# Per-token sums of squares: blocks of 32 ones stand still, the squares move through four column strips, the sums pass through memory as rows

## Chip, cores and metric

One core of one Trainium2 chip. The metric is the device time of one execution in microseconds (us), the median of the runs shown; fewer is better.

## The reference

One layer of a decoder trunk on 1024 tokens of width 1024: a gated mixer branch, a Mamba-2 (SSD) branch, and a merge of both. What matters here is the end of the SSD branch. Its output `y_b`, 2048 values per token, is multiplied with a gate and then normalised in 8 groups of 256 values, each by the root of its own mean square:

```python
y_b = ssd_scan(xh, dt, a, bm, cm) + xh * d_skip[:, None]
yz = (y_b.reshape(b, s, SSM_D_INNER) * silu(ssm_z)).reshape(b, s, SSM_GROUPS, 256)
y_b = rms_norm(yz, ssm_norm_w.reshape(SSM_GROUPS, -1))    # yz * rsqrt(mean(yz*yz) + EPS) * w
merged = sigmoid(g_a) * (y_a @ w_proj_a) + sigmoid(g_b) * (y_b @ w_proj_b)
return x + gate * (merged @ w_out)
```

So for each of the 8 groups and each of the 1024 tokens one number is wanted: the inverse root of a mean of 256 squares.

## The kernel before

Activations lie transposed: 128 channels on the partitions, tokens along a row. A group of 256 channels is a tile `yz` of two halves j, each 128 channels by 512 tokens, and there are two such tiles per group, q = 0 and 1 (first and second 512 tokens).

The SSD stage runs 32 steps. `order` lists them as pairs of groups that take turns: (0,0), (1,0), (0,1), (1,1) and so on, four steps s of 256 tokens per group, then the next pair of groups. A step has three items, `front`, `back` and `prep`, and after each item `run_tasks` starts whatever was put off with `later(delay, ...)` for that many items. Between the items, matrix products of another branch (`proj_a`, tiles `pma`) are drawn in to fill TensorE. `fetch` loads the next step's `sl` and `dcy`; there are 5 sets of these buffers. Matmuls (`mm`, L81), transposes (`tp`, L84) and the loads on the SP queue (`load`, L90) keep the order in which they are written; stores go out on ScalarE's queue (`store`, L93) and these, with the instructions of VectorE (V), ScalarE (A) and GpSimd (G), are placed by a scheduler that works by its own estimate of times.

After every second step of a group, `post` (L1078) stores `yz` to `yb_d`, puts off `squares` by 5 items (in place: ScalarE squares both halves, GpSimd adds them) and `post2` by 17. `post2` (L1098) sums over the 128 channels on TensorE: each 128x128 block of squares is loaded as weights and one column of ones moves through it, so that the tokens come out on the partitions, one column per block, and L1104 makes the mean and adds EPS for 128x4 values into `ssq`. After the second half L1108 takes the power -0.5 of the group's 8 columns on GpSimd. Eight items later `post3` (L1112) transposes these 8 columns on TensorE into 8 rows, VectorE copies them out, and a store writes them to `rs_d`.

Groups 6 and 7 end last. Their second halves are done beside the first product `p1` of the next stage: `late.post2` follows unit 1 and unit 4 of `p1` with both halves of the squares unadded (tiles `sq`, so 16 instead of 8 matmul instructions), and `post3` follows units 4 and 6. There, `rows_bank` hands out the accumulators `yp` that the product `p5` takes over afterwards.

The next stage multiplies the normalised `y_b` with `w_proj_b` in units of 12 matmuls, order p1, p5, p2, p3, p6, p7, p4. `y_load` broadcasts `rs_d` to `rb` and loads `yb_d` to `yn`, 6 units ahead; `y_norm` (L1403) and the splits (L1442 to L1448) follow 4 units ahead.

One more place uses narrow weights already, at the start of the kernel, in `matvec` (tile `pm`): 32-wide weights, written to four strips of 32 partitions:

```python
mm(pm[32 * q : 32 * q + 32, 0:256], scz[:, i, :], aw[n][:, i].rearrange("p j c -> p (j c)"), i < 4, i >= 4)
```

In the trace a float32 matmul shows as two instructions (two passes).

Of the kernel before, what the change touches and what calls it, by code (L numbers as in the profile page):

```python
# [12 lines left out]
ALU = mybir.AluOpType  # L13
# [3 lines left out]
P = 128  # L17
D = 1024
S = 1024
KT = D // P  # L20
NCH = S // P
NG = 8
# [3 lines left out]
EPS = 1e-6  # L26
# [9 lines left out]
def hybrid_kernel(  # L36
# [7 lines left out]
    V, A, G, PE = nc.vector, nc.scalar, nc.gpsimd, nc.tensor  # L44
# [8 lines left out]
    def dt_(shape, name):  # L53
        return dram.tile(shape, F32, name=name, tag=name)

    acs_d = dt_([NG, 4, HPG, 256], "acs_d")
    rs_d = [dt_([1, S], f"rs_d{g}") for g in range(NG)]
    v_d = dt_([NG, P, NCH * P], "v_d")
    ya_d = [dt_([P, S], f"ya_d{g}") for g in range(NG)]
    mt_d = [dt_([P, S], f"mt_d{g}") for g in range(NG)]  # L60
# [9 lines left out]
    def cst(shape, name, dt=F32):  # L70
        return const.tile(shape, dt, name=name, tag=name)
# [8 lines left out]
    def mm(acc, l, r, first=True, last=True):  # L80
        pin(PE.matmul(acc, l, r, start=first, stop=last))  # L81

    def tp(dst, src, idn):
        pin(PE.transpose(dst, src, idn))  # L84
# [4 lines left out]
    def load(dst, src):  # L89
        pin(nc.sync.dma_start(dst, src))  # L90

    def store(dst, src):
        nc.scalar.dma_start(dst, src)  # L93

    ident = cst([P, P], "ident")
    make_identity(nc, ident)
    ones = cst([P, P], "ones")
    G.memset(ones, 1.0)
    tri = cst([P, P], "tri")
    G.affine_select(out=tri, in_=ones, compare_op=ALU.is_ge, fill=0.0, base=0,  # L100
                    pattern=[[1, P]], channel_multiplier=-1)
    nhalf = cst([P, NCH], "nhalf")
# [13 lines left out]
    cwt = cst([P, P], "cwt")  # L116
# [9 lines left out]
    ssq = cst([P, NG * NCH + 24], "ssq")  # L126
# [356 lines left out]
    def later(delay, f, *a):  # L483
        tasks.append((slot[0] + delay, f, a))
# [474 lines left out]
    class Group:  # L959
# [136 lines left out]
            G.tensor_add(sq[0], sq[0], sq[1])  # L1096

        def post2(self, q, sq):  # L1098
            g = self.g
            pq = rows_bank[0](f"pq{g}_{q}")  # L1100
            for i in range(4):
                for j, t in enumerate(sq):
                    mm(pq[:, i : i + 1], t[:, i * P : (i + 1) * P], ones[:, 0:1], j == 0, j == len(sq) - 1)
            V.tensor_scalar(ssq[:, g * NCH + q * 4 : g * NCH + q * 4 + 4], pq[:, 0:4], 1.0 / 256, EPS,  # L1104
                            op0=ALU.mult, op1=ALU.add)
            if q == 1:
                c8 = slice(g * NCH, (g + 1) * NCH)
                G.tensor_tensor(ssq[:, c8], ssq[:, c8], nhalf, op=ALU.pow)  # L1108
                if g < NG - 2:
                    later(8, self.post3)  # L1110

        def post3(self):  # L1112

            g = self.g
            pr = rows_bank[0](f"pr{g}")
            tp(pr[0:NCH, 0:P], ssq[:, g * NCH : (g + 1) * NCH], ident)
            row = (cwt, tri)[g % 2][0:NCH, :]
            V.tensor_copy(row, pr[0:NCH, 0:P])
            store(rs_d[g].rearrange("o (c p) -> (o c) p", p=P), row)

    groups = [Group(g) for g in range(NG)]
    rows_bank = [bank]
# [233 lines left out]
    def banks(name, c):  # L1356
        return [psb.tile([P, 512], F32, name=f"{name}{j}", tag=f"b{c}{j}") for j in range(4)]
# [99 lines left out]
    def multiply(u, ps):  # L1457
        nm, k = units[u]
        first = nm in ("p1", "p5", "p2", "p3")
        a, (bh, bl) = aops.pop(u), bops.pop(u)  # L1460
        for j in range(4):
            js = slice(j * P, (j + 1) * P)
            for n, (v, r) in enumerate(((0, bh), (0, bl), (1, bh))):
                pin(PE.matmul(ps[j], a[:, v, js], r, start=first and n + k == 0, stop=n == 2 and k == KT - 1,  # L1464
                              skip_group_check=not first))
# [3 lines left out]
    def gate_load(b, h):  # L1469
        hs = slice(h * 512, (h + 1) * 512)  # L1470
        th, ma = gate_slot(f"tg{b}_{h}"), gate_slot(f"ma{b}_{h}")
        load(th, th_d[(KT + b) * P : (KT + b + 1) * P, hs])
        load(ma, mt_d[b][:, hs])
        gates[b, h] = th, ma
# [105 lines left out]
    for u, (nm, k) in enumerate(units):  # L1580
        if k == 0:
            if nm == "p1":
                psy = banks("yp5", "y")
                psx = banks("x", "x")
                rows_bank[0] = lambda name: psy[("pr6", "pr7", "pq6_1", "pq7_1").index(name)]
            elif nm in ("p2", "p3"):
                psy = banks(f"y{nm}", "y")
            elif nm == "p6":
                room.extend(rb_r[0])
            ps = psy if nm in ("p2", "p5", "p3") else psx  # L1590
        multiply(u, ps)
        ahead(u)
        if nm == "p1" and k in (1, 4):
            late = groups[NG - 2 + k // 4]
            late.post2(1, late.late)
        if nm == "p1" and k == 4:
            for tags, _ in (y1_r, ym_r):
                room.extend(tags)
        if nm == "p1" and k in (4, 6):
            groups[NG - 4 + k // 2].post3()  # L1600
        if k % 2 and nm in GATES:
            gate_load(GATES[nm][0] + k // 2, GATES[nm][1])
        if nm == "p4":
            for at, f, a in BESIDE:
                if at == k:
                    f(*a)
        if k % 2 and more and nm not in ("p2", "p5"):
            merged(*more.pop(0))
        if k == KT - 1:
            for j in range(4):  # L1610
                with tc.high_priority():
                    if nm == "p1":
                        t = slot_tile(f"c11_{j}")
                        A.copy(t, psx[j])
                        more.append((j, 0, t, f"c11_{j}"))
# [184 lines left out]
```

## Time and profile before

| | |
|---|---|
| time, median of 3 runs | 1409.17 us (1408.26 to 1411.2) |
| profiled execution, its own time | 1411.01 us |
| its span | 1409.2 us |
| TensorE busy / VectorE / ScalarE / GpSimd | 98% / 75% / 57% / 15% of the span |
| granted TensorE clock, mean | 0.998 |
| SSD stage in the trace | about 950 to 1162 us |
| product p1 | 1162 to 1189 us |

Busy time of TensorE counts overlapping matmuls once, and the ends of matmuls are modelled; the distance from one start to the next says more. PE is TensorE's matmuls, PEld its weight loads, DVE is VectorE, ACT ScalarE, POOL GpSimd, and SPq and ACTq are the queues on which SyncE and ScalarE issue transfers.

### The profile page before, as it was taken

To read this page: it belongs to the slowest core of one execution; us is meant where nothing else is said; L and a number is where in the kernel's file an instruction comes from. 1 tells how busy PE (TensorE), PEld (TensorE's weight loads), DVE (VectorE), ACT (ScalarE), POOL (GpSimd) and SP (SyncE) were. 2 spreads that over 40 slices of the span, in tenths; PEclk is the share of its full clock that TensorE was granted. 3 is DMA by queue.
4 is the path that set the end of the run, shared out by engine and by line. 5 is a ranking of instruction groups with operands and counts; after the bars stand their busy time and mean duration, and the time that the engine had idled before them with its cause. 6 is when DMAs were issued, how large, how long until landed. Compare 5 with 4: busy or idle time off the path is not lost. (4 is left out here: it accounts for less than half of the span.)

```text
span 1409.2 us, 20659 instructions
## 1 busy us (share of the span) xinstructions
PE 1380.6 (98%) x7051; PEld 1146.3 (81%) x7051; DVE 1061.2 (75%) x1863; ACT 796.5 (57%) x1471; POOL 213.7 (15%) x208
## 2 busy tenths in 40 slices
PE   8999999999999999999999999999999999999997
PEld 6788888888888888888888888888887887878886
DVE  4686677767868899788898786378677757875976
ACT  5664576656566655555566555586776723322443
POOL 0000000000000011000100010037778850000001
PEclk9999999999999999999999999999999999999999
DMA  8552433333444667877766874498788759878903
GB/s 265 150 162 82 148 98 107 110 109 105 131 136 141 179 198 238 256 232 229 219 196 175 250 221 120 165 337 310 260 283 278 268 193 333 322 232 296 359 26 120
DMA packets 271918, 283.13 MB, mean 201 GB/s; under 512 B 14300, under 2 KB 222596, under 8 KB 271812
## 3 DMA queue, kind: packets, MB, share of 16 engines
q1 hardware_dynamic: 184548, 198.39, 44.1%
q10 hardware_dynamic: 87264, 83.41, 17.6%
q8 instruction: 56, 0.92, 0.3%
q14 instruction: 50, 0.41, 0.1%
HBM read 194.42 MB, written 87.33 MB: 200 GB/s over the span
## 5 line engine op out<-in xcount | busy, mean ns | idle before, releaser
L780 POOL TENSOR_TENSOR wog<-wog,gb 128x256 f32<-128x256 f32 x16 | 18.0, 1140 | 672.4 <-DMA wog<-in_w_out_dram 672.4
L994 ACT ACTIVATE dcy<-dcy,nacs 128x128 f32<-128x128 f32 x256 | 78.6, 388 | 15.5 <-POOL dcy L989 14.5
L989 POOL TENSOR_SCALAR_AFFINE_SELECT dcy<-dcy 128x1024 f32<-128x1024 f32 x32 | 35.4, 1105 | 139.6 <-ACT ea L986 135.8
L907 ACT ACTIVATE ac<-ac 128x1024 f32<-128x1024 f32 x32 | 33.9, 1060 | 25.0 <-DVE ac L905 24.8
L986 ACT ACTIVATE ea<-dcy 64x512 f32<-64x512 f32 x64 | 40.1, 626 | 13.7 <-DMA dcy<-acs_d 13.3
L81 PE MATMUL pma<-yh,wah 128*128 128x512 f32 x128 | 43.3, 419 | 0.0
L81 PE MATMUL pma<-yh,wal 128*128 128x512 f32 x128 | 42.6, 413 | 0.0
L1076 POOL TENSOR_TENSOR yz<-y,sl 128x512 f32<-128x512 f32 x32 | 41.4, 1293 | 1.1
L1014 DVE TENSOR_TENSOR dcy<-dcy,pc 128x1024 f32<-128x1024 f32 x32 | 38.9, 1216 | 3.3 <-PE pc L84 1.9
L81 PE MATMUL pma<-yl,wah 128*128 128x512 f32 x128 | 40.1, 394 | 0.0
L1074 DVE TENSOR_TENSOR ym<-yn,ea 128x512 f32<-128x512 f32 (+1 forms) x32 | 19.9, 621 | 26.6 <-PE yn L81 26.5
L1075 POOL TENSOR_TENSOR y<-y,ym 128x512 f32<-128x512 f32 (+1 forms) x32 | 36.6, 1142 | 13.6 <-DVE ym L1074 13.5
L81 PEld LDWEIGHTS yn<-sl,st 128*128 128x128 f32 x224 | 30.4, 190 | 9.0 <-POOL yz L1076 3.6
L81 PE MATMUL yn<-sl,st 128*128 128x128 f32 x224 | 31.7, 277 | 5.5 <-DVE st L1044 5.5
L905 DVE SCALAR_TENSOR_TENSOR ac<-c2x,cwt,ac 128x1023 f32<-128x1023 f32 (+2 forms) x24 | 31.2, 1299 | 5.7 <-ACT ac L903 5.6
L81 PE MATMUL sp<-xe,bn 128*128 128x256 f32 x112 | 32.6, 408 | 2.7 <-DVE xe L1010 1.2
L81 PE MATMUL yi<-dcy,xd 128*64 128x128 f32 x512 | 35.0, 279 | 0.2 <-DVE st L1044 0.2
L1403 DVE SCALAR_TENSOR_TENSOR yn<-yn,par,rb 128x512 f32<-128x512 f32 x32 | 23.9, 747 | 14.5 <-DMA yn<-yb_d 14.4
L905 DVE SCALAR_TENSOR_TENSOR ac<-c2cb,cwt,ac 128x1023 f32<-128x1023 f32 (+2 forms) x24 | 31.2, 1298 | 4.5 <-ACT ac L903 4.3
L1678 POOL TENSOR_TENSOR r<-r,fnw 128x512 f32<-128x512 f32 x2 | 2.6, 1298 | 203.8 <-DMA out_dram<-r 203.8
L1042 POOL TENSOR_TENSOR st<-st,cd 128x256 f32<-128x256 f32 x48 | 32.0, 666 | 5.9 <-PE yn L81 4.6
L905 DVE SCALAR_TENSOR_TENSOR ac<-c1cb,cwt,ac 128x1023 f32<-128x1023 f32 (+2 forms) x24 | 31.1, 1296 | 1.4 <-ACT ac L903 1.4
(2977 smaller groups left out, 4396.2 us busy)
## 6 DMA issues: line engine op xcount, KB each, us to landing
sl<-s_d SPq DMA_DIRECT2D x32, 768.0 KB, 4.7
s_d<-ac ACTq DMA_DIRECT2D x32, 512.0 KB, 4.3
dcy<-acs_d SPq DMA_DIRECT2D x32, 512.0 KB, 9.3
aw<-in_ada_w_dram SPq DMA_DIRECT2D x16, 512.0 KB, 3.7
wbr<-in_w_proj_b_dram SPq DMA_DIRECT2D x64, 128.0 KB, 4.6
wb_d<-wbb ACTq DMA_DIRECT2D x32, 256.0 KB, 4.9
wb_d<-wbc ACTq DMA_DIRECT2D x32, 256.0 KB, 3.3
yb_d<-yz ACTq DMA_DIRECT2D x32, 256.0 KB, 6.0
```

Of the source, the lines that this page charges most:

```text
L81: pin(PE.matmul(acc, l, r, start=first, stop=last))
L905: V.scalar_tensor_tensor(ac[:, s:], cc[:, : S - s], conv_wt[:, 3 - s, i : i + 1], ac[:, s:], op0=ALU.mult, op1=ALU.add)
L907: A.activation(ac, ac, AF.Silu)
L986: A.activation(ea[hh * HD : (hh + 1) * HD], dcy.rearrange("p (j e) i l -> p e j (i l)", e=2)[hh * HD : (hh + 1) * HD, hh], AF.Exp)
L989: G.affine_select(out=d8, in_=d8, compare_op=ALU.is_ge, fill=-1e30, base=0, pattern=[[0, 2 * HPG], [1, P]], channel_multiplier=-1)
L994: A.activation(dcy[:, h, i, :], dcy[:, h, i, :], AF.Exp, bias=sub[:, i, h : h + 1])
L1014: V.tensor_tensor(d3, d3, pc[:, 0:256].unsqueeze(1).to_broadcast([P, HPG, 256]), op=ALU.mult)
L1042: G.tensor_mul(v3(s2), v3(self.st), fac(cd, g, s)[:, i].unsqueeze(2).to_broadcast([P, HPG, HD]))
L1074: V.tensor_tensor(m[:, :, t0:], yn.rearrange("p (j l) -> p j l", j=2)[:, :, t0:], ea[:, :, t0:], op=ALU.mult)
L1075: G.tensor_add(y1[:, :, t0:], y1[:, :, t0:], m[:, :, t0:])
L1076: G.tensor_mul(yz, y1, sl[:, 4:6])
L1403: V.scalar_tensor_tensor(t, t, snw[:, n : n + 1], rbs[n // 2, h], op0=ALU.mult, op1=ALU.mult)
```

## The change

`post2` turns the roles round. A block of 32 columns of ones is the weight, the squares are what moves, and each of the four blocks of 128 tokens goes to its own strip of 32 output partitions. The sums come out as rows (each 32 times over). VectorE makes mean plus EPS of all 128x128 values into `cwt` (first half) or `tri` (second half), and a store writes rows 0, 32, 64 and 96 to a new piece of memory, `ms_d`. `post3` loads the group's 1024 means back as 128 partitions of 8 neighbouring tokens and takes the power there; a new `post4`, four items later, stores the result to `rs_d`. The transposes through the identity and the copies of the 8 rows go. For groups 6 and 7 `post3` stays behind units 4 and 6 of `p1`, and `post4` follows units 5 and 7.

```diff
         def post2(self, q, sq):
             pq = rows_bank[0](f"pq{g}_{q}")
-            for i in range(4):
-                for j, t in enumerate(sq):
-                    mm(pq[:, i : i + 1], t[:, i * P : (i + 1) * P], ones[:, 0:1], j == 0, j == len(sq) - 1)
-            V.tensor_scalar(ssq[:, g * NCH + q * 4 : g * NCH + q * 4 + 4], pq[:, 0:4], 1.0 / 256, EPS,
-                            op0=ALU.mult, op1=ALU.add)
-            if q == 1:
-                c8 = slice(g * NCH, (g + 1) * NCH)
-                G.tensor_tensor(ssq[:, c8], ssq[:, c8], nhalf, op=ALU.pow)
-                if g < NG - 2:
-                    later(8, self.post3)
+            for j, t in enumerate(sq):
+                for i in range(4):
+                    mm(pq[32 * i : 32 * i + 32, 0:P], ones[:, 0:32], t[:, i * P : (i + 1) * P], j == 0, j == len(sq) - 1)
+            row = (cwt, tri)[q]
+            V.tensor_scalar(row, pq[:, 0:P], 1.0 / 256, EPS, op0=ALU.mult, op1=ALU.add)
+            store(ms_d[g][:, q * 512 : (q + 1) * 512].rearrange("o (i p) -> (o i) p", p=P), row[0:P:32, :])
+            if q == 1 and g < NG - 2:
+                later(8, self.post3)

         def post3(self):
-            pr = rows_bank[0](f"pr{g}")
-            tp(pr[0:NCH, 0:P], ssq[:, g * NCH : (g + 1) * NCH], ident)
-            row = (cwt, tri)[g % 2][0:NCH, :]
-            V.tensor_copy(row, pr[0:NCH, 0:P])
-            store(rs_d[g].rearrange("o (c p) -> (o c) p", p=P), row)
+            c8 = ssq[:, g * NCH : (g + 1) * NCH]
+            load(c8, ms_d[g].rearrange("o (p c) -> (o p) c", p=P))
+            G.tensor_tensor(c8, c8, nhalf, op=ALU.pow)
+            if g < NG - 2:
+                later(4, self.post4)
+
+        def post4(self):
+            c8 = ssq[:, g * NCH : (g + 1) * NCH]
+            store(rs_d[g].rearrange("o (p c) -> (o p) c", p=P), c8)
...
-                rows_bank[0] = lambda name: psy[("pr6", "pr7", "pq6_1", "pq7_1").index(name)]
+                rows_bank[0] = lambda name: psy[("pq6_1", "pq7_1").index(name)]
...
         if nm == "p1" and k in (4, 6):
             groups[NG - 4 + k // 2].post3()
+        if nm == "p1" and k in (5, 7):
+            groups[NG - 4 + k // 2].post4()
```

More of the change, by code (lines that the diff above doesn't have):

```diff
@@ L57, in hybrid_kernel @@
     rs_d = [dt_([1, S], f"rs_d{g}") for g in range(NG)]
+    ms_d = [dt_([1, S], f"ms_d{g}") for g in range(NG)]
     v_d = dt_([NG, P, NCH * P], "v_d")
@@ L1100, in post2 @@
             pq = rows_bank[0](f"pq{g}_{q}")
-            for i in range(4):
-                for j, t in enumerate(sq):
-                    mm(pq[:, i : i + 1], t[:, i * P : (i + 1) * P], ones[:, 0:1], j == 0, j == len(sq) - 1)
-            V.tensor_scalar(ssq[:, g * NCH + q * 4 : g * NCH + q * 4 + 4], pq[:, 0:4], 1.0 / 256, EPS,
-                            op0=ALU.mult, op1=ALU.add)
-            if q == 1:
-                c8 = slice(g * NCH, (g + 1) * NCH)
-                G.tensor_tensor(ssq[:, c8], ssq[:, c8], nhalf, op=ALU.pow)
-                if g < NG - 2:
-                    later(8, self.post3)
+            for j, t in enumerate(sq):
[6 more added lines that the diff above has]
+                later(8, self.post3)
         def post3(self):
             g = self.g
-            pr = rows_bank[0](f"pr{g}")
-            tp(pr[0:NCH, 0:P], ssq[:, g * NCH : (g + 1) * NCH], ident)
-            row = (cwt, tri)[g % 2][0:NCH, :]
-            V.tensor_copy(row, pr[0:NCH, 0:P])
-            store(rs_d[g].rearrange("o (c p) -> (o c) p", p=P), row)
+            c8 = ssq[:, g * NCH : (g + 1) * NCH]
[4 more added lines that the diff above has]
+        def post4(self):
+            g = self.g
+            c8 = ssq[:, g * NCH : (g + 1) * NCH]
+            store(rs_d[g].rearrange("o (p c) -> (o p) c", p=P), c8)
     groups = [Group(g) for g in range(NG)]
```

## The prediction

> **What bounds the kernel now.** I read the page's head, then the busy times of the two stretches that the change touches, then who TensorE waits for there.
>
> ```profile
> span 1409.2 us, 20659 instructions
> PE 1380.6 (98%) x7051; PEld 1146.3 (81%) x7051; DVE 1061.2 (75%) x1863; ACT 796.5 (57%) x1471; POOL 213.7 (15%) x208
> ...
> 980.00:1160.00 180.00, 170.75 (x1290) 148.70 (x1289) 127.00 (x236) 111.08 (x286) 134.68 (x130) 1.00 0.75 260
> 1162.00:1190.00 28.00, 26.84 (x135) 22.09 (x134) 21.37 (x37) 9.34 (x17) 3.28 (x2) 1.00 0.92 317
> ...
> PE yn L81 <- DVE st L1044: 5.5, 4, 2.1
> PE sp L81 <- DVE xe L1010: 1.2, 2, 0.6
> PE sp L81 <- DVE ssq L1104: 1.0, 1, 1.0
> PE pq L81 <- DVE st L1044: 0.7, 1, 0.7
> ```
>
> The windows give length, then PE, PEld, DVE, ACT, POOL. In the SSD stretch (980 to 1160) TensorE works 170.75 of 180 us at full clock: it is the bound, with 9.25 us of waits, most of them on VectorE. GpSimd, 15% over the span, is busy for 134.68 of these 180 us: 75%, so 45 us idle in all. In `p1` (1162 to 1190) TensorE lacks 1.2 us and GpSimd has almost nothing to do. TensorE time saved here should therefore count, except where the next TensorE wait eats it.
>
> **The sums on TensorE (saves).** The groups, by tile, and the PE timeline:
>
> ```profile
> L81 PE MATMUL pq<-ones,yz x112: 164/250/271, 987.2 to 1155.0; 128*128 128x1 f32 x112
> L81 PE MATMUL yp<-ones,sq x32: 164/250/250, 1168.7 to 1180.3; 128*128 128x1 f32 x32
> ...
> 980.89 0.27 PE L84 MATMUL pc<-ident,sl 128*128 128x128 f32 x1
> 981.00 0.38 PE L84 MATMUL px<-ident,sl 128*128 128x128 f32 x2
> 981.31 1.09 PE L81 MATMUL yi<-dcy,xd 128*64 128x128 f32 x16
> ...
> 986.96 0.38 PE L84 MATMUL px<-ident,sl 128*128 128x128 f32 x2
> 987.18 0.95 PE L81 MATMUL pq<-ones,yz 128*128 128x1 f32 x8
> 988.06 1.09 PE L81 MATMUL yi<-dcy,xd 128*64 128x128 f32 x16
> 989.78 0.45 PE L81 MATMUL sp<-xe,bn 128*128 128x256 f32 x1 [0.63 <-DVE xe L1010]
> ...
> 1168.21 0.39 PE L1464 MATMUL x<-p1bl,p1a 128*128 128x512 f32 x1
> 1168.44 0.39 PE L1464 MATMUL x<-p1bh,p1a 128*128 128x512 f32 x1
> 1168.66 1.84 PE L81 MATMUL yp<-ones,sq 128*128 128x1 f32 x16
> 1170.37 0.49 PE L1464 MATMUL x<-p1bh,p1a 128*128 128x512 f32 x1
> ...
> 25.23 1.07 PE L81 MATMUL pm<-aw,scz 128*32 128x256 f32 x16
> 26.23 0.38 PE L81 MATMUL acc<-ones,ident 128*128 128x128 f32 x1
> ```
>
> 112 instructions of `pq` are 14 posts of 8; 32 of `yp` are the two late ones of 16. Though one column moves, each instruction costs its weight load: from `pq` to `yi` 988.06 - 987.18 = 0.88 us for 8, 0.11 each. With the last two `px` ahead of it the path from `px` to `yi` is 988.06 - 986.96 = 1.10 us; without a post it is 981.31 - 981.00 = 0.31. The new form is `matvec`'s: 32-wide weights, four strips, 16 instructions, of 256 columns, in 26.23 - 25.23 = 1.00 us. A full-width stream of 128 columns takes 0.11 (981.00 - 980.89), so 256 columns 0.22, and 16 in a row would be 3.5 us: they run four at a time, four rounds of 0.22 = 0.88, and 0.12 for leaving the strips. The new post is two rounds of 128 columns, 0.22; with the 0.31 of entering a narrow form and 0.12 for leaving it the path is 0.65 instead of 1.10: 0.45 saved. A late post is four rounds of 0.11 = 0.44, plus 0.12, plus 0.09 for entering (0.31 less the two 0.11 of `px`): 0.65 against 1170.37 - 1168.66 = 1.71, so 1.06 saved.
>
> [...]
>
> How much of the 14 x 0.45 = 6.3 us arrives? Three posts stand right before a wait of `sp` that does not move with them: `xe` twice and `ssq` once. At 989.78 `sp` waits for VectorE's `xe`, whose input `px` was done before the post began, so a shorter post only lengthens the wait. Four posts lie in the steps ahead of the two longest waits of `yn` (2.1 us each), on VectorE's `st`; there I count half. That leaves 7 x 0.45 + 4 x 0.22 = 4.0 us. The two late posts stand between products of `p1`: 2.1 us.
>
> **The transposes and copies that go.**
>
> ```profile
> L84 PE MATMUL pr<-ident,ssq x6: 271/272/273, 1036.2 to 1149.7; 128*8 128x128 f32 x6
> 1186.45 0.27 PE L84 MATMUL yp<-ident,ssq 128*8 128x128 f32 x1 [0.34 <-POOL ssq L1108]
> L1118 DVE COPY cwt<-pr x3: 268/269/270, 1037.1 to 1144.6; 8x128 f32<-8x128 f32 x3
> L416 DVE COPY cwt<-pp x1: 280/280/280, 57.4 to 57.4; 128x128 f32<-128x128 f32 x1
> L1104 DVE TENSOR_SCALAR ssq<-pq x14: 148/151/160, 989.6 to 1155.7; 128x4 f32<-128x4 f32 x14
> L93 ACTq DMA_DIRECT2D rs_d<-cwt x4: 292/292/297, 1037.4 to 1184.9; - x4
> ```
>
> Eight transposes at 0.11 of stream and the 0.34 us that the last one waits for GpSimd: 1.2 us. VectorE: 16 evacuations grow from 0.15 us towards the 0.28 of a 128x128 copy, 2.1 us more, and 8 copies of 0.27 go, 2.2 us less: nothing in the sum. ScalarE issues 16 stores more, 16 x 0.29 = 4.7 us, on an engine idle for 69 of the 180 us; behind a store that waits for VectorE's row stand its `dcy` exponentials, as they do today behind the store of `rs_d`. If that cover fails, 4.7 us is the most. Consecutive groups now write the same `cwt` or `tri`, so a row waits until the last store has read it; posts of a pair lie a step (6 us) apart, and I count nothing.
>
> **The new wait on memory (costs).** The power no longer follows VectorE's evacuation but a load, and `rs_d`'s store on ScalarE follows the power.
>
> ```profile
> L1108 POOL TENSOR_TENSOR ssq<-ssq,nhalf x8: 1629/1646/1661, 1019.7 to 1184.8; 128x8 f32<-128x8 f32 x8
> 1035.37 0.61 POOL L1042 TENSOR_TENSOR st<-st,cd 128x256 f32<-128x256 f32 x1
> 1037.22 1.28 POOL L1075 TENSOR_TENSOR y<-y,ym 128x512 f32<-128x512 f32 x1 [1.24 <-DVE ym L1074]
> 1039.51 1.29 POOL L1076 TENSOR_TENSOR yz<-y,sl 128x512 f32<-128x512 f32 x1
> 1043.25 1.27 POOL L1075 TENSOR_TENSOR y<-y,ym 128x512 f32<-128x512 f32 x1 [2.45 <-DVE ym L1074]
> ...
> 1034.21 0.32 SPq L90 DMA_DIRECT2D sl<-s_d  x1
> 1034.69 0.32 SPq L90 DMA_DIRECT2D dcy<-acs_d  x1
> ...
> dcy<-acs_d SPq DMA_DIRECT2D x32, 512.0 KB, 9.3
> ACT yz L1095 <- DMA yb_d<-yz: 12.7, 11, 2.5
> ```
>
> `post3` keeps its place, near 1036 us for group 0 (the first `pr`). Its load then goes out on SP right behind `sl` and `dcy` of 1034.2 and 1034.7, which with 9.3 us to landing keep the 16 engines busy ahead of it. On GpSimd `y`, `yz` and `st` queue behind a power that waits, and for them the next `yn` and the next fetch. Bounds for one wait: nothing, if the power is placed behind the transfer (GpSimd idles 2.45 us before 1043.25, room for its 1.65), and the 9.3 us of `dcy`. The nearest row is ScalarE's squares, which the schedule places ahead of the end of their `yb_d` store: 12.7 us in 11 waits, 1.2 each. I take 1.2 for each of the 6 powers in the SSD stretch, 7 us of GpSimd, and pass on a fifth, as 9.25 us of TensorE waits stand beside 45 us of GpSimd idle: 1.5 us.
>
> ```profile
> L1104 DVE TENSOR_SCALAR ssq<-yp x2: 150/152/154, 1171.2 to 1184.5; 128x4 f32<-128x4 f32 x2
> 1178.15 0.32 SPq L90 DMA_DIRECT2D p5a<-wb_d  x1
> ```
>
> In `p1`, group 7's load stands on SP behind the `p5a` of unit 12 (1178.15), but its mean is made only at 1184.5 today and has to land first: SP, with all loads of units 13 and on, may be held for 6.4 us and that landing, and ScalarE's casts for `p5` behind the store of `rs_d`. Cover: TensorE reaches unit 13 near 1203 (`p1` ends and unit 8 begins at 1189, and a unit is 12 x 0.23 = 2.8 us, by 1168.44 - 1168.21). If it fails, the cost is up to the 2.1 us won there and more; I take 0.6.
>
> **Sum.** 4.0 + 2.1 + 1.2 - 1.5 - 0.6 = 5.2 us less. The profiled execution took 1411.0 (span 1409.2): 1405.8 on its terms. It lies 1.8 above the median of 1409.2, from which the forecast is 1404.0.
>
> **Rivals.**
> *The gain is swallowed.* VectorE, ScalarE and GpSimd set the pace of a step, and every shorter post lengthens the next wait. For it: `sp` waiting on `xe`. Against it: only 9.25 us of waits in 180. Only the late posts, less the 0.6, would stay: 1407.7. Chance 0.14.
> *Slower: GpSimd stands still before the power.* The place is the four powers of groups 0 to 3, while fetches run. If each is put right behind `st` (1035.98) and its load lands behind `dcy`, near 1044, it waits 8 us, of which 1.24 + 2.45 = 3.7 are idle today; 4 us each, 16 us of delayed `yz`, of which I pass on two thirds to TensorE, since the step then hangs on GpSimd: 10.7 less the gain of 7.3, and with the 0.6, 1413.2. It decides once a wait passes 3.7 us. For it: 75% busy and the 9.3; against it: the free place at 1040.8. Chance 0.30.
> *The change does not do what it says: the strips run one after another.* Eight instructions of 0.11 and two switches cost what the post costs now, or 0.1 more: 14 x 0.1 + 2 x 0.2 - 1.2 and the waits of 2.1 give 1412. Against it: `matvec`'s 1.00 us. Chance 0.06, of which 0.04 lie within 0.2%.
>
> **How the numbers follow.** Forecast 0.50, rivals 0.14, 0.30 and 0.06. About 0.2%, or 2.8 us, is what a measurement of this kernel can tell from no change. Faster by more: 0.50; within: 0.14 + 0.04 = 0.18; slower by more: 0.30 + 0.02 = 0.32. Range: below, all of 6.3 + 2.1 + 1.2 = 9.6 and no cost, 1399.6, and a little for the power leaving a crowded place, 1398.5; above, the slower rival with a little to spare, 1414.0.
>
> **What would show it.** `pq` as 128*32 with 128 columns, about 0.35 us from its start to `yi`; no `pr`; a late post of about 0.65; TensorE's busy time about 9 us less; GpSimd's wait for the load of `ssq` at about 1.2 us, and not over 3.7; TensorE's waits in the SSD stretch at about 12. Wrong if `pq` still takes 0.8 us, if GpSimd waits 4 us and more for that load, or if TensorE's waits grow by as much as its work shrinks.

## Result and the profile after

The changed kernel takes 1422.65 us (median of 6 runs, 1419.99 to 1424.18) against 1410.15 (6 runs, 1408.26 to 1411.62): a ratio of 1.0084, 95% interval 1.0070 to 1.0098, so about 12 us slower. The forecast was 5 us faster; the time lies above its range.

The page's head, then the two stretches of the windows view that the prediction showed (length, PE, PEld, DVE, ACT, POOL, granted clock, DMA share, GB/s), then whom TensorE waits for from 980 to 1160 us, and from 1160 to 1420 (total, times, longest):

```profile
span 1421.2 us, 20668 instructions
PE 1380.0 (97%) x7043; PEld 1136.8 (80%) x7043; DVE 1062.2 (75%) x1855; ACT 794.7 (56%) x1471; POOL 214.4 (15%) x208
...
980.00:1160.00 180.00, 163.72 (x1264) 136.00 (x1262) 124.70 (x225) 108.81 (x283) 133.89 (x130) 0.97 0.73 249
1162.00:1190.00 28.00, 25.72 (x132) 19.97 (x131) 19.95 (x32) 9.26 (x17) 2.15 (x1) 0.94 0.87 296
...
PE sp L82 <- DVE xe L1011: 6.0, 4, 2.6
PE yi L82 <- DVE st L1045: 2.7, 1, 2.7
PE sp L82 <- DVE ym L1075: 2.6, 1, 2.6
...
PE yp L1470 <- ACT p L1628: 4.1, 1, 4.1
PE x L1470 <- DVE tha L1301: 2.3, 1, 2.3
```

Before, TensorE was busy for 170.75 of the 180 us; now for 163.72. In a stretch of fixed length idle time grows by just what busy time loses, so these two rows alone do not say what became of the saved time; the balance below does. The clock column, 1.00 before, reads 0.97 and 0.94. The longest waits are longer: single ones of 2.6 and 2.7 us from 980 to 1160, where before none was over 2.1, and one of 4.1 later.

Did the sums themselves get shorter? One group row, and the timeline of TensorE around a post of the SSD stage and a late one:

```profile
L82 PE MATMUL pq<-yz,ones x112: 272/285/297, 987.2 to 1159.7; 128*32 128x128 f32 x112
...
986.92 0.38 PE L85 MATMUL px<-ident,sl 128*128 128x128 f32 x2
987.23 0.42 PE L82 MATMUL pq<-yz,ones 128*32 128x128 f32 x8
987.59 1.09 PE L82 MATMUL yi<-dcy,xd 128*64 128x128 f32 x16
989.75 0.45 PE L82 MATMUL sp<-xe,bn 128*128 128x256 f32 x1 [1.06 <-DVE xe L1011]
...
1176.59 0.64 PE L82 MATMUL yp<-sq,ones 128*32 128x128 f32 x16
1177.16 0.50 PE L1470 MATMUL x<-p1bh,p1a 128*128 128x512 f32 x1
```

They did. From `px` to `yi` it is 987.59 - 986.92 = 0.67 us (0.65 predicted, 1.10 before), from `pq` to `yi` 0.36 (0.35 predicted), and a late post takes 0.57 (0.65 predicted, 1.71 before). The next line shows where the first saving went: `sp` now waits 1.06 us for `xe`, 0.43 more than before, which is what the post lost. The prediction had left this post out of its count for that reason; that most of the others would not arrive either is what it missed.

**The balance.** The stretch from the first product of the SSD stage to the start of the output product holds the whole difference (from there to the end of the last matmul it takes 76.5 us before and 76.4 after). Its three parts, SSD stage, `p1`, and `p5` to `p4`, in the windows view of the kernel before, and then of the one after:

```profile
928.60:1162.10 233.50, 224.19 (x1654) 193.59 (x1652) 172.97 (x315) 152.61 (x390) 167.32 (x162) 1.00 0.79 272
1162.10:1189.30 27.20, 26.04 (x131) 21.47 (x130) 21.08 (x36) 8.88 (x15) 3.28 (x2) 1.00 0.92 315
1189.30:1323.80 134.50, 132.20 (x578) 107.59 (x578) 101.79 (x163) 42.42 (x72) 0.00 (x0) 1.00 0.84 298
```

```profile
928.70:1166.90 238.20, 221.87 (x1648) 184.83 (x1647) 173.98 (x309) 150.84 (x388) 166.33 (x162) 0.98 0.77 265
1166.90:1194.50 27.60, 25.32 (x130) 19.65 (x129) 18.96 (x31) 9.34 (x16) 2.15 (x1) 0.94 0.80 271
1194.50:1335.70 141.20, 134.71 (x578) 109.17 (x577) 103.81 (x167) 41.70 (x72) 1.65 (x1) 0.98 0.84 294
```

Length less PE is idle: 12.8 us before, 25.1 after, 12.3 more. The clock below 1.00 comes from six windows of 3.41 us at half clock, 20.5 us in all, in which TensorE was busy for 18.0: by the clock column half of that, 9.0, is lost (from 1221.14 to 1224.98, in one of them, a product of 512 columns starts every 0.43 us; from 1225.89 on, at full clock, every 0.23). What is left, TensorE's work counted at full clock, is 382.4 before and 407.0 - 25.1 - 9.0 = 372.8 after (sums made before rounding). So 9.6 us of work went, close to what the change saves by the prediction's own terms (6.3, 2.1, and 0.9 of the 1.2, whose other 0.3 was a wait), and 12.3 + 9.0 us came in their place: 11.7 us longer. In the SSD stage alone idle time grew by 7.0 us (9.3 to 16.3) while work fell by 7.2, and half clock took 4.9: the stage is 4.7 us longer.

**Where the half clock comes from.** Five windows of the changed kernel, each beginning on the grid of 3.41 us on which the clock changes, and then two of the kernel before, with its most idle one first:

```profile
1078.67:1082.08 3.41, 1.32 (x6) 1.21 (x7) 3.10 (x7) 3.41 (x12) 3.41 (x4) 1.00 0.37 135
1082.08:1085.49 3.41, 3.41 (x10) 2.66 (x9) 1.53 (x3) 2.78 (x7) 1.12 (x2) 0.50 0.64 210
1085.49:1088.90 3.41, 3.41 (x36) 3.04 (x36) 2.24 (x3) 2.39 (x8) 2.64 (x3) 1.00 0.92 281
...
1215.20:1218.61 3.41, 1.22 (x6) 0.68 (x4) 3.41 (x6) 1.76 (x3) 0.00 (x0) 1.00 0.98 351
1218.61:1225.44 6.83, 4.89 (x12) 3.83 (x13) 5.40 (x9) 3.60 (x7) 0.00 (x0) 0.50 1.02 380
```

```profile
1085.84:1089.25 3.41, 2.15 (x12) 1.68 (x10) 3.41 (x7) 1.92 (x7) 3.33 (x3) 1.00 1.03 356
1089.25:1092.66 3.41, 2.59 (x29) 2.43 (x31) 2.43 (x6) 0.00 (x0) 2.31 (x3) 1.00 1.05 403
```

From 1078.67 TensorE is idle for 2.1 of 3.41 us, and the next window runs at 0.50. In the kernel before the most idle window of this stretch lacks 1.3 us, and the clock stays at 1.00. In this execution that kernel has no half-clock window in the whole stretch; the changed one has six, after five idle windows of 2.1 to 2.5 us. The grid is read from the trace: the ten changes of this kernel's clock from 1030.88 to 1225.44 us lie whole multiples of 3.413 us apart. A window idle for 2.1 of its 3.41 us was enough.

The 9.0 us are bookkeeping for one execution, and not by themselves the price of the halving. Of the six executions of the changed kernel three had a mean granted clock of 0.990 to 0.992 (the one shown: 0.991) and three of 0.995 or 0.996. By 1422 us x 0.004 that is an estimated 6 us less at the higher clock, but they took 1420.0 to 1423.3 us against 1422.4 to 1424.2, only 1.5 less in the mean. In the kernel before, run again beside the experiments, a lower clock goes with more time: 1416.4 us in the mean of three executions at 0.994, 1409.9 in that of 36 at 0.998. So how much of the 12 us the halving costs in the changed kernel stays open; the 12.3 us of idle time outweigh the 9.6 us saved without it.

### The profile page after: what moved, and what is told of

It is laid out like the page before. It is cut to its first block, busy times and chain, and to the rows that moved or that the text cites. A ratio compares the mean times of both kernels' runs of the same rounds, so it can differ in the third digit from the quotient of the medians.

```text
span 1421.2 us, 20668 instructions
## 1 busy us (share of the span) xinstructions
PE 1380.0 (97%) x7043; PEld 1136.8 (80%) x7043; DVE 1062.2 (75%) x1855; ACT 794.7 (56%) x1471; POOL 214.4 (15%) x208
## 5 line engine op out<-in xcount | busy, mean ns | idle before, releaser
L82 PEld LDWEIGHTS yi<-dcy,xd 128*64 128x64 f32 x512 | 28.0, 139 | 8.8 <-issue 4.3
```

## Experiments

Each table gives the median, the ratio to the kernel before run beside it with its 95% interval, and the balance in us for the same stretch as above: its length, TensorE's idle time, the loss to half clock and the work. Before: 395.2, 12.8, 0, 382.4; after: 407.0, 25.1, 9.0, 372.8. The balance is that of the one profiled execution.

### First: which part of the change costs

`e1_rows_direct` leaves out the power: the rows of means are stored straight to `rs_d`, with no load and no second store.

```diff
-            store(ms_d[g][:, q * 512 : (q + 1) * 512]...
-            if q == 1 and g < NG - 2: later(8, self.post3)
+            store(rs_d[g][:, q * 512 : (q + 1) * 512]...
```

> The changed kernel without the way through memory: the rows go straight to rs_d, and there is no load, no power and no second store. It leaves out the power -0.5 (rs_d holds the means). Theory Q (queues: stores on ScalarE's queue that wait for a row or for the power, and loads on SP that wait for such a store, hold what stands behind them, until TensorE's waits come in pieces of over 2 us and the granted clock is halved after them): with two of the three gone it is faster than before, 1402 to 1406, with no or one half-clock stretch. Theory S (shorter sums: TensorE's saved time only lengthens its waits for VectorE, past the length at which the clock halves): the sums are as short, so 1418 to 1424 with four or more half-clock stretches. Theory A (accident: any edit makes the schedule fall out anew, by some us either way): anything between 1404 and 1420.

`e2_trip_only` has the sums and transposes of the kernel before and only the trip: rows of means to `ms_d`, load, power, store. The transposes start 4 items earlier for it, in `p1` behind units 2 and 5, and the store follows 4 items behind the load.

```diff
+            store(ms_d[g].rearrange("o (c p) -> (o c) p", p=P), row)   # after the transpose
+            load(c8, ms_d[g]...); G.tensor_tensor(c8, c8, nhalf, op=ALU.pow); store(rs_d[g]..., c8)
```

> The kernel before with the way through memory alone: sums with one moving column of ones and the transposes as before, but the rows hold the means, go to ms_d, come back as 128x8, get the power and are stored to rs_d. Theory Q: slower than before by 5 to 12 us, 1415 to 1422, with half-clock stretches, ScalarE and SP waiting for ms_d, rs_d or the power. Theory S: sums as long as before, so 1407 to 1412. Theory A: anything between 1404 and 1420.

`e3_late_in_p1` moves group 7's `post3` and `post4` to behind units 2 and 4 of `p5`.

```diff
-        if nm == "p1" and k in (4, 6): groups[NG - 4 + k // 2].post3()   # group 7 at k == 6
+        if nm == "p5" and k == 2: groups[NG - 1].post3()
```

> The changed kernel, but group 7's load, power and store follow units 2 and 4 of p5 instead of units 6 and 7 of p1, so that the load of the means does not stand on SP ahead of its store. Theory Q: SP is no longer held for about 10 us there, the wait of 4.1 us at the first p2 matmul and the half-clock stretch of 6.8 us behind it go: 7 us less than the changed kernel, 1414 to 1417, with the loss in the SSD stage left. Theories S and A: the tail's loss is not from this load, 1420 to 1424.

`e4_stores_on_sp` issues the stores to `ms_d` and `rs_d` on SP, not ScalarE.

```diff
-            store(ms_d[g]...
+            nc.sync.dma_start(ms_d[g]...        # rs_d likewise
```

> The changed kernel with the stores to ms_d and rs_d issued on SP's queue instead of ScalarE's, nothing else. Theory Q with ScalarE's queue as the culprit: the squares, casts and exponentials behind those stores come on time, the SSD stage loses its 5 us: 1414 to 1418. Theory Q with SP as the culprit: as slow or slower, 1421 to 1426. Theory S: 1420 to 1424.

| | median | ratio | length | idle | lost to clock | work |
|---|---|---|---|---|---|---|
| e1_rows_direct | 1416.23 | 1.0043 (1.0028 to 1.0058) | 401.1 | 20.8 | 8.0 | 372.4 |
| e2_trip_only | 1424.32 | 1.0106 (1.0082 to 1.0130) | 408.5 | 20.5 | 5.7 | 382.3 |
| e3_late_in_p1 | 1422.14 | 1.0083 (1.0055 to 1.0111) | 405.8 | 27.8 | 4.7 | 373.2 |
| e4_stores_on_sp | 1419.53 | 1.0061 (1.0041 to 1.0080) | 400.2 | 22.4 | 4.8 | 372.9 |

The trip alone costs 15 us (e2; of its 13.3 in the balance 6.3 lie in `p1`, 33.5 us long where it was 27.2). The short sums alone, with nothing new to wait for but the rows' stores, cost 7 (e1), although 10 us of work have gone. The two do not add up to the 12.5 of the whole change, so its parts can't be priced one by one. With the stores moved off ScalarE 12.5 over the kernel before becomes 10.4, but the intervals overlap, so this gain is not clear of noise. e3 missed: SP no longer stood before group 7's load in `p1`, but the time stayed, and TensorE's wait at the start of `p2` grew from 4.1 to 7.4 us.

### Second: the queue of the load, the clock, and what TensorE's time is worth

`f1_load_on_pool` sends the load of the means through GpSimd's queue; all else is the changed kernel.

```diff
-            load(c8, ms_d[g].rearrange("o (p c) -> (o p) c", p=P))
+            nc.gpsimd.dma_start(c8, ms_d[g].rearrange("o (p c) -> (o p) c", p=P))
```

> The changed kernel with the load of the means issued on GpSimd's queue, where the power stands behind it, instead of SP's; nothing else. Theory Q for the part behind p1 (SP held by this load for 11 us, so the loads of p2 late, ScalarE late with clearing p5's accumulators, a wait of 4.1 us and 6.8 us at half clock): from the start of p5 to the first product of the last stage 134 to 136 us as before instead of 141, so 1415 to 1417. Theory A: still 139 to 143 there, 1420 to 1424.

`f2_short_waits` and `f3_long_waits` are the kernel before with waits planted in `p6`, `p7` and `p4`: a product, a copy of its result on ScalarE, and a product that needs the copy; twelve times, or four times with four products on GpSimd in between.

```diff
+        if nm in ("p6", "p7", "p4") and k % 2:          # f3: four places
+            mm(psy[0][:, 0:P], ident, ones)
+            A.copy(cd[:, 0:P], psy[0][:, 0:P])          # f3: and 4 x G.tensor_mul
+            mm(psy[1][:, 0:P], cd[:, 0:P], ones)
```

> The kernel before with 12 short waits planted in p6, p7 and p4: a small product, a ScalarE copy of it, and a second product that needs the copy; about 1 us each, 11 to 14 us of TensorE waits in all. Theory C (a wait costs its length, and 3.4 us at half clock more only where TensorE idles some 2 us of a 3.4 us stretch): no half-clock stretch, the time goes up by the waits and the added products alone, 1420 to 1427. Rival (half clock follows from the sum of the waits): half-clock stretches here as in the next kernel.

> The kernel before with 4 long waits planted in the same products: the copy is followed by four GpSimd products of 0.6 us, so about 3.3 us each, 12 to 14 us of waits in all, as in the kernel with 12 short ones. Theory C: each is followed by a half-clock stretch of 3.4 us or two, so 4 to 8 of them, 7 to 13 us more than the waits: 1428 to 1436, and 5 us or more above the short waits. Rival: as long as the kernel with short waits, within 2 us, or with as few half-clock stretches.

`f4_sums_thrice` is e1 with every sum made three times (it leaves out the power too).

```diff
-            for j, t in enumerate(sq):
+            for j, t in 3 * list(enumerate(sq)):
```

> The kernel with rows stored straight to rs_d (no load, no power, no second store; rs_d holds the means), with each post's sums made three times over in the same strips: TensorE spends about 0.44 us more on each of 14 posts and 0.88 on the two late ones, 8 us in all, so a post lasts nearly as long as before the change. Theory S (the saved time lengthened waits and led to half clock): nothing slower than the same kernel with single sums, 1411 to 1416, waits in the SSD stage back to about 10 us and fewer half-clock stretches. Rival (TensorE is the bound there): 8 us slower than with single sums, 1422 to 1426. Theory A: anything between.

| | median | ratio | length | idle | lost to clock | work |
|---|---|---|---|---|---|---|
| f1_load_on_pool | 1411.75 | 1.0001 (0.9983 to 1.0019) | 395.1 | 18.3 | 4.4 | 372.4 |
| f4_sums_thrice | 1415.71 | 1.0031 (1.0013 to 1.0049) | 401.0 | 16.6 | 3.0 | 381.5 |
| f2_short_waits | 1426.68 | 1.0113 (1.0072 to 1.0154) | | | | |
| f3_long_waits | 1446.05 | 1.0234 (1.0200 to 1.0269) | | | | |

f1: one line takes the whole loss away, though the trip is still made. The forecast had been that only the part behind `p1` would recover (134.8 us from `p5` on, as forecast); the SSD stage recovered too, 230.4 us for 238.1, which was not forecast. f4: 9.1 us of TensorE work on top of e1 cost nothing, because idle fell by 4.2 and the clock's loss by 5.0. In this kernel TensorE's own time beside the SSD stage's waits is worth next to nothing until the waits are covered. The planted waits, f2 first, then f3, and one idle window of f3 with what follows it:

```profile
PE yp L81 <- ACT cd L1596: 8.4, 12, 1.7
...
PE yp L81 <- POOL cd L1599: 23.5, 4, 12.5
...
1297.41:1300.82 3.41, 0.74 (x5) 0.47 (x3) 0.97 (x2) 0.78 (x2) 1.83 (x3) 1.00 1.00 384
1300.82:1307.65 6.83, 5.75 (x15) 4.59 (x16) 0.00 (x0) 0.00 (x0) 0.95 (x2) 0.50 0.27 108
```

Twelve waits of 1.7 us at most gave no half-clock window in these products; four long ones gave 27.3 us of half clock. So the waits make the half clock, and the strips need not be there: f3 makes its sums without them. f3 came out slower than forecast (1428 to 1436), as its waits sum up to 23.5 us, not 12 to 14; with 8.4 against 23.5 us the pair alone does not separate long waits from a larger sum, which the single windows above do. Both traces also have half clock in the SSD stage, 6.83 and 3.41 us, ahead of the planted waits.

### Third: the stores too, more cover, and the hand of chance

`g1_trip_on_pool` is f1 with the stores to `ms_d` and `rs_d` on GpSimd's queue as well. `g2_load_on_pool_fill` is f1 with the products of `proj_a` drawn five at a time, not four and five in turn, so that more of them stand early in the SSD stage; `g4_before_fill` has the same draw in the kernel before. `g3_neutral_delay` is the kernel before with `post3` put off by 9 items, not 8, to see how far a harmless edit moves the time.

```diff
-            draw(6 if n == 2 else 4 + n % 2)
+            draw(6 if n == 2 else 5)            # g2, g4
-            later(8, self.post3)
+            later(9, self.post3)                # g3
```

> The changed kernel with the load of the means and both stores on GpSimd's queue, so that neither SP nor ScalarE ever waits for the way through memory. Theory Q (both queues held): as the kernel with the load alone moved, or better, within 0 to 6 us below the kernel before, ratio 0.996 to 1.000. Rival (only SP counts, and GpSimd, three quarters busy in the SSD stage, pays for 24 more transfers): ratio 1.001 to 1.006.

> The kernel with the load on GpSimd's queue, and 5 products of the other branch drawn in at every step of the SSD stage from step 3 on instead of 4 and 5 in turn, about 15 of them earlier in all, none more. Theory S (waits on VectorE set the pace of a step, TensorE has time to spare): the added products lie in the waits, the SSD stage ends as early or up to 4 us earlier, with fewer half-clock stretches: ratio 0.996 to 1.000. Rival (TensorE is the bound and order does not matter): ratio 1.000, waits as before.

> The kernel before with post3 put off by 9 items instead of 8: no work more or less. Theory A (every edit makes the schedule fall out anew): ratio anywhere from 0.996 to 1.006, and where it is over 1.002, waits of 2 us and half-clock stretches in the SSD stage that the kernel before has not. Theories Q and S: 0.999 to 1.001.

> The kernel before with the same 15 products drawn in earlier, nothing else. Theory S: part of its 9 us of waits in the SSD stage is covered, ratio 0.996 to 1.000. Rival (with longer sums there is no time to spare, the added products delay what VectorE waits for): ratio 1.001 to 1.006.

| | median | ratio | length | idle | lost to clock | work |
|---|---|---|---|---|---|---|
| g1_trip_on_pool | 1416.60 | 1.0054 (1.0035 to 1.0073) | 399.5 | 20.3 | 6.4 | 372.7 |
| g2_load_on_pool_fill | 1408.44 | 0.9979 (0.9964 to 0.9995) | 390.3 | 14.7 | 3.2 | 372.4 |
| g3_neutral_delay | 1410.14 | 1.0008 (0.9990 to 1.0025) | 395.2 | 13.1 | 0.0 | 382.1 |
| g4_before_fill | 1424.47 | 1.0103 (1.0077 to 1.0130) | 407.8 | 18.9 | 7.4 | 381.4 |

g1 came out as its rival said. g2 is 0.2% faster than the kernel before (2.5 us in the median): with the waits better covered, part of the 10 us saved arrives, 4.8 us in the balance. g3 does not support the idea that any edit shifts the schedule by ten microseconds. But in g4 the same draw costs 14 us where the long sums stay, more than its rival allowed; why was not followed up. So an edit that adds no work and touches no queue can cost as much as the whole loss, and the order in which a schedule happens to fall remains a rival for differences between these kernels.

### Fourth: which of the two places of the load

`h1_pool_load_ssd` has the load on GpSimd's queue for groups 0 to 5 (SSD stage) and on SP for groups 6 and 7 (`p1`); `h2_pool_load_p1` has it the other way round.

```diff
+            if g < NG - 2:                       # h2: g >= NG - 2
+                nc.gpsimd.dma_start(c8, ms_d[g]...)
+            else:
+                load(c8, ms_d[g]...)
```

> The changed kernel, in which the load of the means goes out on GpSimd's queue for groups 0 to 5 (SSD stage) and stays on SP for groups 6 and 7 (beside p1). Between the two kernels that have it all on SP and all on GpSimd, the SSD stage ends 7.9 us apart (1166.9 and 1159.0) and the part from p5 on is 141.2 and 134.9. Theory A, SP held by a load that waits for a store, in two places that add up: the SSD stage ends near 1159, TensorE idle in it near 11; from p5 on near 141; time about 6 us over the kernel before (1.004). Theory B, only the hold in the SSD stage matters (the later part follows from how the earlier ends): about the kernel before, within 2 us. Theory C, the loss is the way the schedule happens to fall and not SP: no split by place, anything between 0 and +14, and the wait of SP in p1 does not go with the length from p5 on.

> The reverse: the load of the means on SP for groups 0 to 5, on GpSimd's queue for groups 6 and 7. Theory A: the SSD stage ends near 1167, TensorE idle in it near 16; from p5 on near 135; time about 7 us over the kernel before (1.005). Theory B: as the changed kernel, about 12 us over (1.008). Theory C: no split by place.

`i1_load_later_12` and `i2_load_later_15` keep SP and put `post3` off by 12 and 15 items (SSD stage).

```diff
-                later(8, self.post3)
+                later(12, self.post3)            # i2: 15
```

> The changed kernel with the load of the means put off by 12 items behind the sums instead of 8 (SSD stage, groups 0 to 5), still on SP. In the changed kernel SP stands from 1125.57 to 1131.69 and from 1133.04 to 1138.58 before two of these loads, as the stores of their means are issued only at 1129.84 and 1137.00. Four items are some 8 us, so the means should lie in memory by then. Theory A, these stands are what costs in the SSD stage: the wait of SP for ms_d in the SSD stage falls from 7.4 to near nothing, the idle of TensorE in the stage from 16.3 towards 11, time 1 to 8 us over the kernel before. Theory C, the load on SP costs through what the schedule makes of it, wherever it stands: the wait goes, the time stays near 12 over.

> The same with 15 items. Theory A: as with 12, unless the rows of groups 4 and 5 now come late for the product p1 or behind its loads; 1 to 8 us over the kernel before. Theory C: near 12 over, and no order between 12 and 15.

`j1_extra_sp_load` is h1 with a load on SP at each of the six places in addition, of other data that nobody reads. `j2_load_no_wait` is the changed kernel with the load of groups 0 to 5 taken from those data (it leaves out the means there).

```diff
+                load(ssq[:, 7 * NCH : 8 * NCH], final_norm_w...)                  # j1, beside GpSimd's
-            load(c8, ms_d[g]...)
+            load(c8, final_norm_w... if g < NG - 2 else ms_d[g]...)               # j2
```

> The kernel of h1 (means of groups 0 to 5 loaded through GpSimd's queue, time that of the kernel before) with six more loads on SP at the same places, each of 1024 weights that have lain in memory since the start, into columns that nobody reads. They wait for no store and nothing waits for them. Theory C1, a further transfer in SP's order is what costs: the loss comes back, 6 to 12 us over the kernel before, idle of TensorE in the SSD stage near 16. Theory A1, it costs through its dependence (SP stands for the store, or the power behind it): time stays within 3 us of the kernel before, idle near 12.

> The changed kernel in which the load of groups 0 to 5, on SP at its place, takes 1024 weights that have lain in memory since the start, not the means; so the six powers and all that follows have other numbers, and SP has no store to wait for there. The power still waits for the load. Theory A1: the loss of the SSD stage goes, time within 3 us of the kernel before, idle of TensorE in the stage near 11. Theory C1: it stays, 6 to 12 us over.

| | median | ratio | length | SSD stage | idle | lost to clock | work |
|---|---|---|---|---|---|---|---|
| (after) | 1422.65 | 1.0084 (1.0070 to 1.0098) | 407.0 | 238.1 | 25.1 | 9.0 | 372.8 |
| h1_pool_load_ssd | 1409.82 | 0.9987 (0.9976 to 0.9997) | 392.3 | 229.1 | 17.2 | 2.7 | 372.4 |
| h2_pool_load_p1 | 1417.04 | 1.0044 (1.0029 to 1.0059) | 403.8 | 237.4 | 22.4 | 8.2 | 373.2 |
| i1_load_later_12 | 1417.70 | 1.0039 (1.0024 to 1.0055) | 402.6 | 239.1 | 23.7 | 6.2 | 372.8 |
| i2_load_later_15 | 1422.73 | 1.0068 (1.0046 to 1.0089) | 409.9 | 240.3 | 27.8 | 9.6 | 372.4 |
| j1_extra_sp_load | 1408.26 | 0.9990 (0.9978 to 1.0002) | 393.4 | 229.1 | 18.0 | 3.4 | 372.0 |
| j2_load_no_wait | 1417.26 | 1.0049 (1.0028 to 1.0071) | 399.9 | 233.5 | 20.5 | 6.7 | 372.7 |

First whom SP waits for in the changed kernel, from 1160 to 1230 and from 1000 to 1165 us, and then its timeline near 1125 to 1140 (start, length):

```profile
SPq L91 <- DMA ms_d<-tri: 11.0, 2, 5.7
...
SPq L91 <- DMA ms_d<-tri: 7.4, 2, 5.5
...
1124.65 0.92 SPq L91 DMA_DIRECT2D tha<-th_d  x2
1131.69 0.32 SPq L91 DMA_DIRECT2D ssq<-ms_d  x1
1132.12 0.92 SPq L91 DMA_DIRECT2D tha<-th_d  x2
1138.58 0.32 SPq L91 DMA_DIRECT2D ssq<-ms_d  x1
1139.01 0.37 SPq L91 DMA_DIRECT2D rb<-rs_d  x1
```

SP stands 6.1 us (from 1125.57) and 5.5 us before these two loads, with `tha`, `rb` and `yn` behind them, and twice more in `p1`. The view puts 7.4 of these us down to the means; for the first 4.2 us of the first stand it names a store of `yb_d`. The eye is drawn to `p1`, where the wait is longest. But in h1 SP stands in `p1` as well, and the loss is gone; the stretch from `p5` on takes 133.5 us there (141.2 in the changed kernel, 134.5 before). SP's wait in h1 from 1155 to 1235 us, and the windows of `p1` and of what follows:

```profile
SPq L91 <- DMA ms_d<-tri: 9.9, 2, 5.3
...
1158.00:1187.80 29.80, 26.23 (x129) 20.37 (x129) 21.66 (x35) 11.12 (x19) 3.58 (x2) 0.89 0.83 277
1187.80:1321.30 133.50, 131.65 (x578) 107.77 (x577) 102.49 (x164) 40.67 (x70) 0.00 (x0) 1.00 0.87 305
```

h2 frees `p1` and keeps 6 us of loss, as theory A forecast (7); h1 frees the SSD stage and keeps none, as theory B did. So the two places do not add up: the load of the SSD stage alone on SP loses 6 us, that of `p1` alone none, both together 12. j1 clears the transfer as such: six more on SP cost nothing. j2 takes SP's wait for the store away and wins some 6 of the 12 us. Its SSD stage takes 233.5 us, between the 238.1 of the changed kernel and the 229.1 of h1 and j1: of those 9.0 us 4.6 go with SP's wait, and 4.4 stay with a power that needs a load kept in SP's written order, or with what comes along with it.

For more than the queue differs. In the SSD stage VectorE and GpSimd do their work in the very same order in the changed kernel and in h2, and in f1 and h1; from the one pair to the other a common sequence covers 95% of VectorE's instructions and 86% of GpSimd's. j2 has VectorE's order of the changed kernel to 99%. Of the kernels that lose, e1, e3, h2, i1, i2 and j2 share 96 to 100% of VectorE's order with the changed kernel (e4 and g1, which move the stores, 95 and 90%). No run moves the load and keeps the order.

On GpSimd's queue the load isn't held to its written place. The groups of the changed kernel and of h1 (duration, first and last start):

```profile
L91 SPq DMA_DIRECT2D ssq<-ms_d x6: 320/375/517, 1036.0 to 1138.6; - x6
```

```profile
L1117 POOL DMA_DIRECT2D ssq<-ms_d x6: 552/604/747, 1029.9 to 1131.4; - x6
```

Group 0's load leaves 6 us earlier, those of groups 2 and 3 leave 16 and 18 us earlier (1075.8 and 1080.3, where SP issued them at 1091.6 and 1098.1). That this is the reason was not isolated. i1 and i2 were poor tests: SP still stood before the means in the SSD stage (4.0 and 9.6 us). i1 came out at 6 us over the kernel before, where theory A had put it, but the idle time of the stage (17.3 and 18.7 us) shows no gain from moving the load.

## Why the prediction was wrong, step by step

- **The sums (6.3 saved, of which 4.0 counted), late posts (2.1), transposes (1.2).** Right in size: 9.6 us of work went. In all thirteen kernels with the short sums made once the work is 9.2 to 10.4 us below that of the kernel before, faster and slower ones alike.
- **"How much arrives".** This step failed first. It let 4.0 of the 6.3 us arrive, and all of the 3.3 of the late posts and transposes. In the runs nothing arrived: idle time in the SSD stage grew by 7.0 us as its work fell by 7.2. The step asked which posts stand right before a wait and let most of the rest count in full. But the waits are VectorE's, and wherever the next `sp`, `yn` or `yi` waits for it, a shorter post lengthens that wait. TensorE's 95% in the stretch did not make it the bound: f4 adds 9.1 us of work to e1 and loses no time, g2 gains when products cover the waits. The rival "The gain is swallowed" had this mechanism, but still ended 1.5 us below the kernel before.
- **What `sp` waits for.** The `xe` in these rows is not its operand. At 989.75 the wait ends with the `xe` of 988.92; the `sp` that starts there reads one of 982.96, a step older. In the built program this `sp` takes the accumulator that held the next step's `px`, and that `xe` is what reads `px` out. So it is in all four waits of `sp` for `xe` in the changed kernel. The two at 1015.84 (1.0 us) and 1080.76 (2.57) are new with the change: before, these two `sp` had other accumulators and did not wait. In f1 and h1 the accumulators are shared in the same places; there `xe` comes earlier at the second, and TensorE waits 0.09 us. A kernel that gives `sp` another accumulator was not run.
- **The clock.** No term of the sum had it. In the balance it is 9.0 us: idle time is not worth its length only; once a window lacks 2 us, the next can lose up to 1.7 more (half of 3.41). The executions at a higher clock bear out only a part of that for the changed kernel (1.5 us).
- **GpSimd's wait for the load (1.5, from 7 us).** Over-sized. The row of the SSD stage, and the rows of VectorE's evacuations and ScalarE's stores:

```profile
POOL ssq L1117 <- DMA ssq<-ms_d: 2.7, 3, 1.6
...
L1107 DVE TENSOR_SCALAR cwt<-pq x8: 281/282/292, 989.5 to 1161.2; 128x128 f32<-128x128 f32 x8
L94 ACTq DMA_DIRECT2D ms_d<-cwt x8: 501/504/587, 992.9 to 1161.8; - x8
```

  2.7 us in three waits, none near 3.7, from which the slower rival was to decide. That the rival had the right side was luck: its reason did not come true.
- **SP's hold in `p1` (0.6).** The length was seen (6.4 and a landing; it was 11.0), the price was not: taking this load off SP too wins 6 us where the SSD stage has its hold (h2 against the changed kernel), and none where it has not (h1 loses nothing). SP's hold in the SSD stage, 7.4 us at 1126 to 1138, was not in the sum at all: I asked what stands behind the load on GpSimd, and hardly what stands behind it on SP. By h1 and f1 the loss goes with the load there; by j2 some 6 us of it go with SP's wait.
- **VectorE (0) and ScalarE (nothing, at most 4.7).** VectorE's 0.28 us came as estimated. A store of four rows holds ScalarE for 0.50 us, not 0.29; moving the stores away won 2 us, not clear of noise (e4). The row that must wait until the last store has read `cwt` was counted at nothing; it held VectorE twice, and TensorE waited right behind (1.41 us at 1052.91, with 0.73 us of TensorE behind, and here the second):

```profile
1110.48 0.29 DVE L1107 TENSOR_SCALAR cwt<-pq 128x128 f32<-128x128 f32 x1 [1.36 <-DMA ms_d<-cwt]
...
1111.94 0.71 PE L82 MATMUL yn<-sl,st 128*128 128x128 f32 x4 [1.11 <-DVE st L1041]
```

- **What would show it.** The prediction named its own refutation: "if TensorE's waits grow by as much as its work shrinks". In the SSD stage they grew by 7.0 us as its work shrank by 7.2. Its two other signs did not come: `pq` takes 0.36 us to `yi`, and no wait of GpSimd for the load in the SSD stage is over 1.7 us.

Open remain three things. e1 has neither load nor power and still loses 7 us; so the load on SP is not the only way in which these waits arise, and there `xe` (8.0 us in four waits) and `tha` (one of 4.7) are late with no load of means on SP. Why a load in SP's order costs beyond SP's wait is read from the times of issue, not shown. And g1, which moves two stores more than f1, stands at 1.0054 where f1 stands at 1.0001. The rival for all three is the order of the instructions. The longest wait of `sp` in the changed kernel shows how it works; the last two lines are the kernel before:

```profile
1077.86 0.42 DVE L1045 TENSOR_TENSOR st<-st,sp 128x256 f32<-128x256 f32 x1 [1.42 <-POOL st L1043]
...
1079.93 0.68 DVE L1011 TENSOR_TENSOR xe<-px,dde 128x512 f32<-128x512 f32 x1
...
1080.76 1.10 PE L82 MATMUL sp<-xe,bn 128*128 128x256 f32 x4 [2.57 <-DVE xe L1011]
...
1078.09 0.68 DVE L1010 TENSOR_TENSOR xe<-px,dde 128x512 f32<-128x512 f32 x1
1078.69 0.41 DVE L1044 TENSOR_TENSOR st<-st,sp 128x256 f32<-128x256 f32 x1
```

VectorE does `st` ahead of `xe` there and stands 1.42 us for GpSimd; before, `xe` came first. The loads of means next to it on SP leave at 1041.3 and 1091.6, and e1, which has none, shows the same order and a wait of 3.5 us at this place.

## What to carry to other kernels

Before counting saved TensorE time, ask for each place which engine the next product waits for: a stage at 95% busy can still take its pace from VectorE, and the saving pays only if there are products to put into the gap (g2). Sum idle time by windows of the clock's grid, not over the stage: in these traces windows that lacked less than 1.45 us never led to half clock, those that lacked 2.0 or more always. Ask of a load that waits for a store what stands behind it in a queue that keeps the written order; another queue (h1, f1) took the loss away with one line. And test a harmless edit or two beside the real ones: g4 moved the time by as much as the change.

## What was not expected of the hardware

How sharply idle windows and half clock go together. In the traces of all 20 kernels, from 900 to 1385 us, of the full-clock windows of 3.41 us on its grid all 44 that lacked 2.0 us or more were followed by half clock, 7 of 12 between 1.75 and 2.0, 2 of 15 between 1.45 and 1.75, and none of some 2700 below that (idle from the modelled ends of matmuls, so to about 0.1 us). A half window was left only by a busy one: all 17 that lacked 0.8 us or more were followed by another, those followed by full clock lacked 0.54 us at most, and f3 stayed at half for 10.24 us through its longest wait. And the strips do run together: 16 instructions of 128 columns took 0.57 us from their first start to the next product's, where 16 in a row at the 0.11 us of a full-width stream (980.89 to 981.00 in the kernel before) would take 1.8.
